# The low part of a conv weight moved from GpSimd to VectorE, and six loads moved behind the next raw weights, in a hybrid attention, Fourier and conv block

## The chip, the core and the metric

The kernel runs on one core of a Trainium2 chip. The core has five engines with instruction queues of their own, which meet only through semaphores: TensorE (PE: matrix products, with a second row PEld for loading the stationary operand), VectorE (DVE), ScalarE (ACT), GpSimd (POOL) and SyncE (SP), from whose queue nearly all DMA transfers are issued. The time is that of one execution on the device, in microseconds (us); lower is better.

## The reference

One layer over 1024 latent tokens and 256 context tokens of width 1024, all in float32, cut to what matters here:

```python
h  = rms_norm(x, g_pre) * (1 + scale) + shift          # latent
hc = rms_norm(ctx, g_pre) * (1 + scale_c) + shift_c     # context
q, k, v, g_a, u_f, g_f, c_a, c_b, g_c, s_a, s_f, s_c = split(h @ w_in)
kc, vc = split((hc @ w_in)[:, 512:1536])
y_a = (neighbourhood_attention(q, k, v, kc, vc, rpb) * silu(g_a)) @ p_attn
y_f = ((real(fft2(u_f)) @ w_four) * silu(g_f)) @ p_four
y_c = (conv_module(c_a, c_b, ...) * silu(g_c)) @ p_conv    # c_a * sigmoid(c_b), depthwise conv of 31 taps, ...
merged = sigmoid(s_a) * y_a + sigmoid(s_f) * y_f + sigmoid(s_c) * y_c
out = x + gate * rms_norm(merged @ w_out, g_post)
```

## The kernel before

Every product is made of three: an operand is split into a high part (rounded, made by ACT as a cast) and a low part (source less high part, a subtraction on POOL or DVE), and `mm3` (L140 to L143) adds high x high (L141), then the two mixed products (L142, L143), in PSUM. `split` (L93) issues one cast and one subtraction. The low part goes to the engine that is named, and to POOL where none is.

**Weights** pass through a queue `wq`. `wreq` and `wcol` enter a weight with the number of pieces `parts` that it is split in and, as `lo`, the engines that make the low parts. `emit_raw` (L108) loads the raw weight into a ring of two buffers (`raw`), `emit_split` writes `whi` and `wlo`, rings of two as well. So a raw load waits until both parts of the weight two places ahead have been made, and the high part of a weight waits until PE has finished the weight two places ahead.

**The stage of the first change** ("border", some 67 to 224 us). PE's order is written out by hand; a scheduler that lists instructions by priority orders ACT, DVE, POOL and SP. PE makes the two Fourier maps (`i_uf`), the second channel tile of the map `c_b` (`i_cb1`, the weight that is changed; its raw buffer is `raw2`, its parts `whi2` and `wlo2`), then the values (`v00`, ...), context keys (`k0`, ...) and the Fourier transform. Into the products of the conv map PE mixes eight pairs of transposes of the context (`tp`, L704); ACT turns each into `h` (L706) and a high part `ch`, POOL makes the low part `cl`. `h` and the transposes have rings of two. Meanwhile DVE runs the depthwise conv: chains of multiply-adds ("taps", L485) with two accumulators, `cacc` (even taps) and `cb_` (odd taps), each 128x512 or 513, joined in L500 to L504. In `fold` (L734, L735) DVE makes `e32` and `o32` from a Fourier map `ut`; ACT and POOL split them (`eh`, `el`, `oh`, `ol`). The weights `wf`, `bc` and `bs` are split by ACT and POOL too (`l_wf`, `l_bc`, `l_bs`). PE multiplies them into four small products, whose low part `wcl` DVE makes; the products take turns in two PSUM buffers, so the third waits for the first `wcl`.

**The stage of the second change** (pairs of gate tiles, about 510 to 745 us). All engines run in the order of the code. Twelve pairs of weight tiles are multiplied with seven products each instead of eight: `step(n, what)` makes the products `p1` to `p7` of pair `n` and the sums `g2`, `g3`, `g4`, `g7`, from which gates are made. `prep_a` to `prep_d` and `wsum` make the stationary operands from the raw weights (`c<-raw` and `w<-raw` in the profile); `raws(n)` loads the two raw tiles of pair `n`, into the same ring of two. `emit_th` writes the tanh of a gate into a ring of two (`th`, L1323) and stores it to DRAM (`thd`, L1324). Pairs 5 to 7 instead multiply their gate into the merge rows `mg[0, 1, 4..7]` (L1340) and store them to `fcd` (L1341). These rows are loaded from `fcd` beforehand: the six loads that are moved, 512 KB each. Up to then the `mg` buffers hold sums of the normalised input (`h_sums`, `h_last`), which are no longer needed at either place.

After the pairs, the branch outputs are projected, merged (`mg`), multiplied with `w_out` and normalised.

Of the kernel before, what the change touches and what calls it, by code (L numbers as in the profile page):

```python
# [19 lines left out]
P = 128  # L20
# [3 lines left out]
KT = D // P  # L24
# [11 lines left out]
Q0, K0, V0, GA0, UF0, GF0, CA0, CB0, GC0, SA0, SF0, SC0 = (  # L36
    0, 512, 1024, 1536, 2048, 2304, 2560, 2816, 3072, 3328, 4352, 5376,
)
# [14 lines left out]
def block_kernel(ctx: ExitStack, tc: tile.TileContext, x, ctxt, wmodp, wgate,  # L53
                 rows2, cols, w_in, rpbp, w_four, w_pw, pst, w_out, masks, bdc, bds, dcos, dsin, out):
    nc = tc.nc
    pe, act, dve, pool, sp = nc.tensor, nc.scalar, nc.vector, nc.gpsimd, nc.sync
# [12 lines left out]
    fcd = dpool.tile([8, P, T], F32, name="fcd")  # L69
# [30 lines left out]
    def wreq(ap, k, n, parts=1, lo=None):  # L100
        wq.append([ap, k, n, None, None, None, parts, lo])
        return len(wq) - 1

    def emit_raw(i):
        while state["raw"] <= min(i, len(wq) - 1):
            e = wq[state["raw"]]
            t = wp.tile([P, e[1], e[2]], F32, tag="raw", bufs=2, name=f"raw{state['raw']}")
            sp.dma_start(t, e[0])  # L108
            e[3] = t
            state["raw"] += 1  # L110
# [26 lines left out]
    def wcol(c0, parts=1):  # L137
        return wreq(w_in[:, c0:c0 + P].rearrange("(k p) c -> p k c", p=P), KT, P, parts)
# [30 lines left out]
    i_s = [[0, 0, 0] for _ in range(8)]  # L169
    i_v, i_kc, i_dft = [[0, 0], [0, 0]], [0] * 4, [[0, 0], [0, 0]]  # L170
    i_uf = [wcol(UF0 + c * P, 4) for c in range(2)]
    i_cb1 = wcol(CB0 + P)
    border = "v00 k0 v01 k1 v10 k2 v11 k3 d0 s0 d1 d2 s1 d3".split()
    for what in border:
        n = int(what[1])
# [1022 lines left out]
    mg = [mgt[d // 4][:, d % 4] for d in range(8)]  # L1198
# [85 lines left out]
    def prep_b(n, which=(0, 1)):  # L1284
        if (n, "c1") not in ops:
            ops[n, "c1"] = [slot(12 + i, f"c1{n}").rearrange("p (k c) -> p k c", k=8) for i in range(2)]
        for i in which:
            put(n, f"s{i + 1}", ops[n, i], ops[n, "c1"], i)
# [13 lines left out]
    def raws(n):  # L1302
        emit_raw(pairs[n - 1][2][1] + 2)
# [135 lines left out]
    def go(n, *what):  # L1439
        for w in what:  # L1440
            step(n, w)
# [40 lines left out]
    go(0, "g7")  # L1482
    h_split(4, 2, 3)
    go(1, "g7")
    for r in (6, 7, 4, 5, 0, 1):
        sp.dma_start(mg[r], fcd[r])
    go(2, "p6", "g2")
    wsum(2, 2)
    wsum(2, 3)
# [12 lines left out]
    prep_d(3)  # L1502
    prep_b(3)
    raws(4)
    go(2, "p3")
    go(3, "p1")
    go(2, "g3")
# [384 lines left out]
```

## Time and profile before

| | us |
|---|---|
| median of 3 runs (930.76 to 933.38) | 930.91 |
| the profiled execution | 931.39 |
| its span, first to last instruction | 929.5 |
| PE busy / DVE busy / ACT busy / POOL busy | 889.4 / 708.3 / 417.3 / 289.4 |
| mean granted TensorE clock | 0.986 of full speed |

How to read the rows. A row of the timeline has start (us from the span's start), duration, engine, line, operation, out<-in by the program's names, shape, count; in brackets the idle time of the engine ahead of it and what released it. Durations of instructions of one engine overlap a little, so that the distance of starts tells the pace. A DVE or POOL instruction's duration holds the time for which it waits after its start. A row of the windows has the stretch and its length, then for PE, PEld, DVE, ACT and POOL busy us and number of instructions, then granted clock, share of the DMA engines in use, GB/s. A row of the waits reads: engine, output and line that waited, releaser; us in total, times, longest.

### The profile page before, as it was taken

Reading aid. Unit: us, or ns where it says so; the run is one execution under the profiler, and the core shown is the slowest. Engines: PE = TensorE matmul, PEld = TensorE weight load, DVE = VectorE, ACT = ScalarE, POOL = GpSimd, SP = SyncE. Lnnn points to the kernel's source line nnn. Section 1 sums busy time; section 2 is a strip of 40 time slices with the busy share of each in tenths; the row PEclk is TensorE's granted clock in tenths of the full one; section 3 lists DMA queues with packets and bytes.
Section 4 is the critical chain, followed back from the end, with each engine's and each line's share of the span. In section 5 each row is a group of like instructions: output and inputs, shape, how many; then the busy total and the mean of one; then the engine's idle time right before and its main releaser. Section 6 shows DMA issues by size and latency. Waiting matters only on the chain. (4 is left out here: it accounts for less than half of the span.)

```text
span 929.5 us, 13195 instructions
## 1 busy us (share of the span) xinstructions
PE 889.4 (96%) x4652; PEld 746.5 (80%) x4652; DVE 708.3 (76%) x1213; ACT 417.3 (45%) x836; POOL 289.4 (31%) x272
## 2 busy tenths in 40 slices
PE   5999999999899999999999999999999999998997
PEld 4677899988678988888888887888888888776685
DVE  5659479582668999999968785667766679998885
ACT  5542523233357676777652544433343530315442
POOL 3026822263234344444521000002300037670232
PEclk9999899999899999999999999999999999999999
DMA  9711133345424554545422238334321798853234
GB/s 367 290 41 68 46 103 126 124 130 180 124 85 141 143 152 127 160 124 143 130 80 91 69 99 281 118 101 125 103 68 46 257 347 311 310 187 104 99 106 136
DMA packets 114163, 135.86 MB, mean 146 GB/s; under 512 B 5681, under 2 KB 83761, under 8 KB 114097
## 3 DMA queue, kind: packets, MB, share of 16 engines
q1 hardware_dynamic: 113952, 134.43, 44.3%
q0 software_dynamic: 144, 0.59, 0.3%
q8 instruction: 37, 0.61, 0.3%
q14 instruction: 30, 0.24, 0.1%
HBM read 102.03 MB, written 29.36 MB: 141 GB/s over the span
## 5 line engine op out<-in xcount | busy, mean ns | idle before, releaser
L141 PE MATMUL ps<-hh,whi 128*128 128x512 f32 x304 | 128.2, 422 | 0.9 <-DVE qd L866 0.9
L93 POOL TENSOR_TENSOR wlo<-raw,whi 128x512 fp32r<-128x512 f32 (+2 forms) x53 | 89.3, 1701 | 117.6 <-ACT whi L93 105.5
L143 PE MATMUL ps<-hh,wlo 128*128 128x512 f32 x304 | 121.0, 398 | 4.7 <-POOL wlo L93 4.7
L142 PE MATMUL ps<-hl,whi 128*128 128x512 f32 x304 | 120.6, 397 | 0.0
L1657 POOL TENSOR_TENSOR mg<-mg,th 128x512 f32<-128x512 f32 x28 | 47.6, 1701 | 99.4 <-DVE th L1654 98.0
L93 ACT CAST whi<-raw 128x512 fp32r<-128x512 f32 (+2 forms) x65 | 43.7, 704 | 74.1 <-PE ps L142 29.7
L143 PEld LDWEIGHTS ps<-hh,wlo 128*128 128x128 f32 x304 | 58.3, 192 | 18.4 <-POOL wlo L93 5.6
L1340 POOL TENSOR_TENSOR mg<-mg,th 128x512 f32<-128x512 f32 x12 | 17.7, 1473 | 167.7 <-DVE th L1339 167.7
L93 DVE TENSOR_TENSOR c<-w,c 128x512 fp32r<-128x512 f32 x64 | 45.9, 756 | 30.4 <-ACT c L93 30.4
L141 PEld LDWEIGHTS ps<-hh,whi 128*128 128x128 f32 x304 | 58.4, 192 | 11.1 <-PE ps L143 1.3
L142 PEld LDWEIGHTS ps<-hl,whi 128*128 128x128 f32 x304 | 58.6, 193 | 9.9 <-issue 0.5
L1028 POOL TENSOR_TENSOR bias<-mk,braw 128x288 f32<-128x288 bf16 (+1 forms) x64 | 54.1, 847 | 38.8 <-DVE mn L1060 37.6
L1093 ACT CAST pt<-tp 96x384 fp32r<-96x384 f32 (+1 forms) x96 | 46.1, 514 | 43.0 <-PE tp L1086 42.1
L1099 DVE TENSOR_TENSOR pt<-tp,pt 96x384 fp32r<-96x384 f32 (+1 forms) x96 | 54.4, 593 | 2.9 <-ACT pt L1093 1.5
L1060 DVE CUSTOM_DVE_ANT_0 pr<-scb,bias 128x544 f32<-128x544 f32 (+1 forms) x64 | 49.4, 772 | 8.4 <-PE scb L1053 7.7
L1067 ACT ACTIVATE pr<-pr,mn 128x544 f32<-128x544 f32 (+1 forms) x64 | 50.8, 794 | 3.7 <-DVE mn L1060 3.6
L143 PE MATMUL ps<-gh,wlo 128*128 128x512 f32 x128 | 50.0, 390 | 0.7 <-DVE wlo L93 0.7
L141 PE MATMUL ps<-gh,whi 128*128 128x512 f32 x128 | 50.3, 393 | 0.0
L142 PE MATMUL ps<-gl,whi 128*128 128x512 f32 x128 | 49.9, 390 | 0.2 <-DVE gl L93 0.2
L1086 PE MATMUL tp<-ident,pr 128*128 128x128 f32 (+1 forms) x320 | 45.8, 274 | 1.4 <-DVE rc L1073 1.0
L93 ACT CAST c<-w 128x512 fp32r<-128x512 f32 x64 | 37.0, 619 | 22.6 <-DVE w L1281 22.3
L1074 DVE TENSOR_SCALAR pr<-pr,rc 128x544 f32<-128x544 f32 (+1 forms) x64 | 41.7, 651 | 2.3
(496 smaller groups left out, 2562.1 us busy)
## 6 DMA issues: line engine op xcount, KB each, us to landing
raw<-in_w_in_dram SPq DMA_DIRECT2D x51, 512.0 KB
wt<-in_wmodp_dram SPq DMA_DIRECT2D x16, 512.0 KB
thd<-th SPq DMA_DIRECT2D x32, 256.0 KB
th<-thd SPq DMA_DIRECT2D x32, 256.0 KB
braw<-in_rpbp_dram SPq DMA_DIRECT2D x32, 192.0 KB
vt<-vd SPq DMA_DIRECT2D x48, 128.0 KB
vd<-vs SPq DMA_DIRECT2D x20, 256.0 KB
vt<-vd SPq DMA_DIRECT2D x48, 96.0 KB
```

The costliest lines, as they stand in the source:

```text
L93: return act.copy(hi, src), (lo_eng or pool).tensor_tensor(out=lo, in0=src, in1=f32(hi), op=ALU.subtract)
L141: pe.matmul(ps, wh, mh, start=start, stop=False, **kw)
L142: pe.matmul(ps, wh, ml, start=False, stop=False, **kw)
L143: pe.matmul(ps, wl, mh, start=False, stop=stop, **kw)
L1028: pool.tensor_tensor(out=dst, in0=mk[:, a * 3 + MJ[j], 0:n].rearrange("p (r w) -> p r w", w=W), in1=raws[h_, min(j, 1)][:, :, 0:W], op=ALU ...
L1060: dve.tensor_tensor_reduce(out=pr, in0=sc, in1=biases[h_][:, FULL[h_](n)], scale=1.0, scalar=BIG, op0=ALU.add, op1=ALU.min, accum_out=mn)
L1067: act.activation(pr, pr, AF.Exp, scale=-1.0, bias=mn, accum_out=sums)
L1074: dve.tensor_scalar(out=pr, in0=pr, scalar1=rc, scalar2=None, op0=ALU.mult)
L1086: pe.transpose(tp[0:(kw if b < 3 else P), b], src, ident)
L1093: act.copy(pt[0:q, b0:b1, 0], tp[0:q, b0:b1])
L1099: dve.tensor_tensor(out=pt[0:q, b0:b1, 1], in0=tp[0:q, b0:b1], in1=f32(pt[0:q, b0:b1, 0]), op=ALU.subtract)
L1657: eng.tensor_tensor(out=mg[d][:, s], in0=mg[d][:, s], in1=t, op=ALU.add)
```

## The change

The low part of the weight `i_cb1` is made by DVE, and both parts in four pieces of 128x256 instead of one of 128x1024. The six loads of merge rows stand behind `raws(4)`.

```diff
     i_uf = [wcol(UF0 + c * P, 4) for c in range(2)]
-    i_cb1 = wcol(CB0 + P)
+    i_cb1 = wreq(w_in[:, CB0 + P:CB0 + 2 * P].rearrange("(k p) c -> p k c", p=P), KT, P, 4, [dve])
...
     go(0, "g7")
     h_split(4, 2, 3)
     go(1, "g7")
-    for r in (6, 7, 4, 5, 0, 1):
-        sp.dma_start(mg[r], fcd[r])
     go(2, "p6", "g2")
     wsum(2, 2)
     wsum(2, 3)
     go(2, "p5")
     prep_c(2)
     go(0, "p4")
     prep_d(2)
     raws(3)
     go(0, "g4")
     go(1, "p4", "g4")
     go(2, "p7")
     prep_a(3)
     go(2, "p4", "g7", "g4")
     for i in range(4):
         wsum(3, i)
     prep_d(3)
     prep_b(3)
     raws(4)
+    for r in (6, 7, 4, 5, 0, 1):
+        sp.dma_start(mg[r], fcd[r])
     go(2, "p3")
```

What the scheduler makes of the first edit on DVE, in the border stage. Before, the two accumulators alternate for a long stretch (twenty rows ahead of these are alike), then come the folds and the second piece of the value weight (`wlo3`):

```order
L485 SCALAR_TENSOR_TENSOR cacc0_696<-u0_694,colt_70,cacc0_696 128x513
L485 SCALAR_TENSOR_TENSOR cb__710<-u0_694,colt_70,cb__710 128x512
L734 TENSOR_TENSOR e32_1064<-ut0_756 128x511
L735 TENSOR_TENSOR o32_1065<-ut0_756 128x511
L93 TENSOR_TENSOR wlo3_971<-raw3_878,whi3_970 128x512
L500 SCALAR_TENSOR_TENSOR cacc0_696<-cacc0_696,colt_70,cb__710 128x512
```

Now five even taps in a row come ahead of the first piece `wlo2`; a tap follows each piece, and the odd taps that are left stand in a row of seven behind the folds (shown from the last piece on):

```order
L485 SCALAR_TENSOR_TENSOR cacc0_696<-u0_694,colt_70,cacc0_696 128x513 x5
L93 TENSOR_TENSOR wlo2_875<-raw2_808,whi2_874 128x256
...
L485 SCALAR_TENSOR_TENSOR cacc0_696<-u0_694,colt_70,cacc0_696 128x513
L485 SCALAR_TENSOR_TENSOR cb__710<-u0_694,colt_70,cb__710 128x512
L734 TENSOR_TENSOR e32_1070<-ut0_756 128x511
L735 TENSOR_TENSOR o32_1071<-ut0_756 128x511
L485 SCALAR_TENSOR_TENSOR cb__710<-u0_694,colt_70,cb__710 128x512 x7
L93 TENSOR_TENSOR wlo3_977<-raw3_884,whi3_976 128x512
```

The number of taps is the same, but seven of them now depend each on the one directly ahead. PE's order is unchanged, POOL only loses the one subtraction, ACT's one cast becomes four with a copy of a Fourier map after the first.

On SP, in the stage of pairs, before (`raw37` and `raw38` are the weights of pair 3, `raw39` and `raw40` those of pair 4):

```order
L1324 DMA thd_59<-th_6166 128x512
L1486 DMA mg1_5659<-fcd_58 128x1024 x4
L1486 DMA mg0_5658<-fcd_58 128x1024 x2
L1324 DMA thd_59<-th_6190 128x512
L108 DMA raw37_6234<-in_w_in_dram 128x8x128
L108 DMA raw38_6236<-in_w_in_dram 128x8x128
L1324 DMA thd_59<-th_6239 128x512
```

and now:

```order
L108 DMA raw37_6234<-in_w_in_dram 128x8x128
L108 DMA raw38_6236<-in_w_in_dram 128x8x128
L1324 DMA thd_59<-th_6239 128x512
L1324 DMA thd_59<-th_6256 128x512
L1324 DMA thd_59<-th_6293 128x512
L1324 DMA thd_59<-th_6297 128x512
L108 DMA raw39_6317<-in_w_in_dram 128x8x128
L108 DMA raw40_6319<-in_w_in_dram 128x8x128
L1504 DMA mg1_5665<-fcd_58 128x1024 x4
L1504 DMA mg0_5664<-fcd_58 128x1024 x2
L1324 DMA thd_59<-th_6355 128x512
L1324 DMA thd_59<-th_6378 128x512
```

Both pairs of raw weights and five tanh stores now go ahead of the six loads; the two tanh stores of the last rows now stand behind them.

## The prediction

> **What bounds the kernel now.** The page comes first: its table of busy time says which engine's time is the kernel's time.
>
> ```profile
> PE 889.4 (96%) x4652; PEld 746.5 (80%) x4652; DVE 708.3 (76%) x1213; ACT 417.3 (45%) x836; POOL 289.4 (31%) x272
> ```
>
> TensorE (PE) is busy for 889 of 929.5 us, so only what makes it wait, or run slowly, can be won. The waits of PE, longest first, are the second view (us in total, times, longest). Two rows touch the change, and a third stands close behind it.
>
> ```profile
> PE ps L143 <- POOL wlo L93: 4.7, 2, 3.8
> PE x L141 <- ACT c L93: 2.9, 2, 1.7
> ...
> PE ps L141 <- DVE wcl L93: 1.0, 1, 1.0
> ```
>
> The third view, the timeline, gives the places. First the wait on `wlo`, on PE:
>
> ```profile
> 88.36 0.38 PE L704 MATMUL tp<-ident,x 128*128 128x128 f32 x2
> 89.99 0.38 PE L704 MATMUL tp<-ident,x 128*128 128x128 f32 x2
> 90.45 0.40 PE L142 MATMUL ps<-hl,whi 128*128 128x512 f32 x1
> 94.68 0.79 PE L143 MATMUL ps<-hh,wlo 128*128 128x512 f32 x1 [3.84 <-POOL wlo L93]
> 100.82 0.40 PE L143 MATMUL ps<-hh,wlo 128*128 128x512 f32 x1
> ```
>
> One round (a pair of context transposes and six products) takes 89.99 - 88.36 = 1.63 us, and a product 0.23. The product at 94.68 was due at 90.68: 4.0 us lost. From 94.68 to 100.82 lie exactly two rounds, 3.26 us of work, and they took 6.14. The windows view gives the reason: the granted clock (the number before the last two) is half there.
>
> ```profile
> 94.68:100.82 6.14, 6.14 (x17) 4.76 (x17) 2.30 (x3) 4.68 (x10) 5.53 (x8) 0.50 0.35 96
> 571.00:575.40 4.40, 4.31 (x11) 3.17 (x12) 4.19 (x7) 2.75 (x6) 0.00 (x0) 0.61 0.46 171
> ```
>
> So the wait cost 4.0 + 2.88 = 6.9 us. Why `wlo` came late stands in the rows of POOL, DVE and ACT.
>
> ```profile
> 79.49 15.13 POOL L93 TENSOR_TENSOR wlo<-raw,whi 128x1024 fp32r<-128x1024 f32 x1 [3.47 <-ACT whi L93]
> 130.25 2.41 POOL L93 TENSOR_TENSOR wlo<-raw,whi 128x1024 fp32r<-128x1024 f32 x1 [2.29 <-ACT whi L93]
> 94.71 1.41 POOL L93 TENSOR_TENSOR cl<-h,ch 128x256 fp32r<-128x256 f32 x2
> 109.15 1.30 POOL L93 TENSOR_TENSOR ol<-o,oh 128x512 fp32r<-128x512 f32 x1
> ...
> 77.88 0.75 DVE L485 SCALAR_TENSOR_TENSOR cacc<-u,colt,cacc 128x513 f32<-128x513 f32 x1
> 91.74 0.69 DVE L735 TENSOR_TENSOR o<-ut 128x511 f32<-128x511 f32 x1
> 98.48 0.71 DVE L93 TENSOR_TENSOR wlo<-raw,whi 128x512 fp32r<-128x512 f32 x1 [6.05 <-ACT whi L93]
> 121.96 0.42 DVE L93 TENSOR_TENSOR wcl<-ps,wch 128x256 fp32r<-128x256 f32 x1
> ...
> 78.36 1.05 ACT L93 CAST whi<-raw 128x1024 fp32r<-128x1024 f32 x1 [3.47 <-issue]
> 95.47 0.56 ACT L706 ACTIVATE h<-tp,mods 128x256 f32<-128x256 f32 x1 [7.29 <-POOL cl L93]
> ```
>
> The same subtraction that takes 2.41 us elsewhere took 15.13 here. It ended 2.2 us after DVE's unbroken row of convolution taps ended (91.74 + 0.69 = 92.43): POOL stood still while DVE ran taps end to start. Where the taps depend on each other the two take turns:
>
> ```profile
> 194.59 1.74 POOL L93 TENSOR_TENSOR wlo<-raw,whi 128x512 fp32r<-128x512 f32 x1
> 195.22 1.66 DVE L485 SCALAR_TENSOR_TENSOR cacc<-u,wsum,cacc 128x512 f32<-128x512 f32 x1
> 156.78 6.28 DVE L485 SCALAR_TENSOR_TENSOR cacc<-u,colt,cacc 128x513 f32<-128x513 f32 x8
> ```
>
> A turn of both takes 1.7 us, of which POOL's 128x512 is 1.25 (1.30 less the overlap with the next) and DVE's tap 0.47. Alone, dependent taps come every 6.28 / 8 = 0.79. The Trainium skill (SBUF — State Buffer, Who interferes with whom) calls this an exclusive lock between GpSimd and VectorE instructions with two SBUF inputs, in which the loser blocks; it speaks against the change, since work moved from one of these engines to the other stays behind the same lock. The trace agrees, in the 15.13 us above.
>
> The second place is PE at 569, where pair 3 of the gate tiles begins:
>
> ```profile
> 569.01 0.39 PE L143 MATMUL z<-hh,c 128*128 128x512 f32 x1
> 571.09 0.50 PE L141 MATMUL x<-hh,c 128*128 128x512 f32 x1 [1.70 <-ACT c L93]
> 575.56 0.39 PE L143 MATMUL x<-hh,c 128*128 128x512 f32 x1
> ...
> 539.73 1.14 ACT L93 CAST c<-raw 128x512 fp32r<-128x512 f32 x2 [0.38 <-DMA raw<-in_w_in_dram]
> 568.70 0.63 ACT L1323 ACTIVATE th<-u 128x512 f32<-128x512 f32 x1 [6.88 <-DMA thd<-th]
> 570.42 1.14 ACT L93 CAST c<-raw 128x512 fp32r<-128x512 f32 x2 [1.09 <-DMA raw<-in_w_in_dram]
> ...
> 535.57 0.99 SPq L108 DMA_DIRECT2D raw<-in_w_in_dram  x2
> 556.84 2.84 SPq L1486 DMA_DIRECT2D mg<-fcd  x6
> 560.38 4.40 SPq L108 DMA_DIRECT2D raw<-in_w_in_dram  x2
> ...
> 560.00:570.00 10.00, 9.40 (x42) 7.46 (x40) 2.52 (x4) 1.26 (x2) 0.00 (x0) 1.00 1.04 358
> ```
>
> The product due at 569.24 began at 571.09 (1.85 lost); eleven products to 575.56 took 4.47 us instead of 11 x 0.23 = 2.5 (1.97 lost, at the clock of 0.61 above). The raw weights it waits for were issued at 560.38 behind the six `mg` loads, with the DMA engines full (share 1.04, the last but one number), and landed 10 us later; without `mg` ahead, those issued at 535.57 were there at 539.7, in 4.1 us. Together 3.8 us.
>
> **Part 1: the weight's low part on DVE.** POOL loses one 128x1024 subtraction, 2.2 us behind the lock. ACT makes the high part in four casts of at most 0.56 (`h` above has 128x256 too), up to 1.2 us more than the one of 1.05, on an engine that waits at this place anyway. The pieces stand behind five chained taps, which from 77.88 at 0.79 each end at 81.8. Instructions that don't depend on the one ahead follow each other at 0.66 (21 from 77.88 to 91.74), a piece of 128x256 at half of that: the four pieces with three taps between them end at 85.1, or, each at its full 0.42 and 0.79, at 85.9. PE needs them from 90.68 on. The wait of 4.0 and its half clock go: 6.9 us. SP gains: its next raw load waited for this subtraction to free its buffer, and comes 9 us earlier; nobody waited for it.
>
> What is late next? Eight more instructions follow on DVE that don't depend on the one ahead (taps and the first fold), at 0.66, to 90.2, and POOL's first `cl` (ready at 86.6) must wait for it. ACT's `h` of round k waits for `cl` of round k-2, as 95.47 shows, and the transpose of round k for `h` of round k-2. With a `cl` of 0.62 and a tap of 0.47 per turn, `cl` 0 to 3 end at 90.8, 91.9, 93.0, 96.4 (a piece of the value weight lies between the last two), and transposes 5 and 7 wait 0.3 and 0.4 us. PE stays 6.9 - 0.7 = 6.2 us ahead, say 6.0 with the semaphores.
>
> But the lock's row decides what follows. From 90.2 until `ol` is done (109.15 + 1.24 = 110.4 before) it must hold, in turns: 13 DVE instructions (six taps, the value weight's piece, one tap, L500, L504, L502, L490, L466) at 0.47 = 6.1, and on POOL eight `cl` at 0.62 (5.0), one value piece (1.25), `l_wf` (1.25), `l_bc` and `l_bs` (0.8), `el` and `ol` (2.5), a short copy (0.1): 10.9. The end is 107.2, only 3.2 earlier. Everything up to `wcl` follows in the old distance: the second fold, its splits, the tanh for the second half of the conv map, the taps. `wcl` then ends at 122.4 - 3.2 = 119.2, and PE is at this product 6.0 earlier:
>
> ```profile
> 121.15 0.28 PE L143 MATMUL ps<-whi,hl 128*128 128x256 f32 x1
> 122.44 0.38 PE L141 MATMUL ps<-h_wf,h_bs 128*128 128x256 f32 x1 [1.01 <-DVE wcl L93]
> ```
>
> It would be due at 121.27 - 6.0 = 115.3 and waits until 119.25: 4.0 us, as long as the wait removed. A wait of that length cost 2.9 us of half clock, which I take again. Part 1: -3.2 + 2.9 = -0.3 us.
> The unknown is the tap's share of a turn. At 0.47 the chain ends 3.2 earlier; at the 0.79 of lone taps the 13 instructions take 10.3 and it ends 1.0 later. The place is like 195.22, so I take 0.47 and keep both: part 1 from -3.2 + 2.9 to +1.0 + 2.9.
>
> **Part 2: the six `mg` loads.** On SP they move behind one tanh store, the raws of pair 3, four tanh stores and the raws of pair 4. They wait for nothing at either place. The raws of pair 3 can then go when their buffers are free: after `w` (558.1) and after `c` (560.5), both on DVE.
>
> ```profile
> 557.43 0.69 DVE L1281 TENSOR_TENSOR w<-raw,w 128x512 f32<-128x512 f32 x1
> 559.86 0.69 DVE L93 TENSOR_TENSOR c<-raw,c 128x512 fp32r<-128x512 f32 x1
> ...
> L1340 POOL TENSOR_TENSOR mg<-mg,th x12: 1289/1414/1681, 619.8 to 675.0; 128x512 f32<-128x512 f32 x12
> ```
>
> In 4.1 us they land at 562.2 and 564.6; ACT's cast (0.6) and DVE's subtraction (0.7) are done by 564, 5 us before PE needs them at 569.24. ACT's wait of 6.88 for a tanh buffer goes too, as that store is no longer behind `mg`. So -3.8 us. What is moved back: the raws of pair 4 go at about 570.5, `mg` from 571.5 on (2.84 to issue, some 9 us to land by the 10 above, so until 584), and two tanh stores behind them land at about 584. ACT takes the first of those buffers again after pair 3's seventh product, at 586: 2 us to spare, and a late tanh there holds up nothing on PE for another 5. `mg` itself is first read at 619.8, 35 us later. Cost nothing.
>
> **Sum.** -0.3 - 3.8 = -4.1 us against the profiled execution (931.39 us, span 929.5, 1.9 around it), that is 927.3. It lies 0.5 over the median of 930.91, to which the same difference gives 926.8.
>
> **Rivals.** (a) PE does not wait for `wcl`: the chain keeps up with PE, part 1 is -6 and the total -10: 921. Against it: 17 us of work behind one lock. (b) It waits as computed, but the clock stays: -3.2 - 3.8 = -7: 924. The wait at 571 pulled the clock down after only 1.7 us, one of 1.0 at 122.44 did not, so this needs a `wcl` wait near 1 us or luck. The Trainium skill (TensorE: Matmul & The Clock Gate, What's actually happening) puts the drop at an idle window of about 3.4 us; by that, a wait shortened to 2 or 3 us would already bring this case. (c) Turns go badly: POOL is held off as at 79.49, the chain is up to 1.0 later, half clock on top: +3.9 - 3.8, about 931, no change. (d) Slower: the half clock after `wcl` outlasts the 6.1 us seen. Each us of it costs 0.47 (2.88 / 6.14); with gains of 7.0 it decides from 15 us on, and at 22 us gives 934. DVE is at its busiest there, which feeds short waits on PE; but the low stretches shown above ended after 6.1 and 4.4 us. (e) The `mg` loads were not what held the raws: part 2 gives nothing, total -0.3: 930.6; against it stand 10 us against 4.1.
>
> **How the numbers follow.** A measurement here can tell about 0.3% (2.8 us) from no change, so faster means under 928.1. The forecast, within 925 to 928.5: 0.47. (a) 0.11; (b) 0.19; (c) 0.14; (d) 0.03; (e) 0.06. Faster: (a), (b) and nine tenths of the forecast, 0.73; slower (d), 0.03; the same 0.24. The range leaves out (d), (e), half of (a) and a third of (c), 0.19 in all: 921.5 to 930.3.
>
> **What would show it.** In the profile after: no PE wait on `wlo` near 91, and four DVE rows `wlo` 128x256 by 86; short PE waits on `h` at the transposes; PE's wait on `wcl` of about 4 us near 119 with a granted clock of 0.5 behind it; `ol` ended near 107. At 569 (less what part 1 moved) no wait and full clock, ACT's `c` waiting for no DMA, the `mg` loads in SP's rows behind the second pair of raws. The prediction is wrong if PE waits for `cl` for more than 2 us, if the `wcl` wait stays at 1 us, or if a tanh buffer stops PE after 580.

## The result, and the profile after

The changed kernel took 926.01 us (median of 14 runs, 924.53 to 930.23), the kernel before 931.36 (14 runs on the same chip, 929.62 to 933.95). The ratio is 0.9948, 95% interval 0.9938 to 0.9958: 0.5% faster, against a forecast of 926.8. The profiled execution took 925.71 us (span 924.0), 5.7 less than the one of before.

From the list of PE's waits after: the wait of 3.8 on the conv weight's `wlo` is gone (the 0.9 left is a later weight's, and stood beside it before), that on `x<-c` of 1.7 too, and the wait on `wcl` has grown from 1.0.

```profile
PE ps L141 <- DVE wcl L93: 5.4, 1, 5.4
...
PE ps L143 <- POOL wlo L93: 0.9, 1, 0.9
```

The timeline after at the first place, by engine (PE, DVE, POOL, ACT). This execution runs 0.64 us later than the one of before up to here (first context transpose at 85.79, before at 85.15), 0.5 of it from a longer first wait of PE.

```profile
85.79 0.38 PE L704 MATMUL tp<-ident,x 128*128 128x128 f32 x2
97.09 0.38 PE L704 MATMUL tp<-ident,x 128*128 128x128 f32 x2
120.52 0.58 PE L141 MATMUL ps<-h_wf,h_bs 128*128 128x256 f32 x1 [5.37 <-DVE wcl L93]
...
85.65 0.42 DVE L93 TENSOR_TENSOR wlo<-raw,whi 128x256 fp32r<-128x256 f32 x1
89.24 1.23 DVE L485 SCALAR_TENSOR_TENSOR cb__710<-u,colt,cb__710 128x512 f32<-128x512 f32 x1
105.43 1.78 DVE L502 SCALAR_TENSOR_TENSOR cacc<-cacc,colt,cb__710 128x512 f32<-128x512 f32 x1
108.40 0.68 DVE L734 TENSOR_TENSOR e<-ut 128x511 f32<-128x511 f32 x1
120.05 0.42 DVE L93 TENSOR_TENSOR wcl<-ps,wch 128x256 fp32r<-128x256 f32 x1
...
87.30 3.77 POOL L93 TENSOR_TENSOR cl<-h,ch 128x256 fp32r<-128x256 f32 x2 [6.89 <-ACT ch L93]
89.88 2.33 POOL L93 TENSOR_TENSOR cl<-h,ch 128x256 fp32r<-128x256 f32 x2
104.90 1.76 POOL L93 TENSOR_TENSOR ol<-o,oh 128x512 fp32r<-128x512 f32 x1
...
109.17 0.62 ACT L93 CAST eh<-e 128x512 fp32r<-128x512 f32 x1 [8.41 <-DVE e L734]
```

The last of the four pieces is done at 86.07. The eight pairs of transposes, 85.79 to 97.09, follow at an even 1.61 us: no wait on `h` at all. The third small product then stands for 5.37 us until `wcl`, which ends at 120.47. The windows view tells what follows: half clock for some five us, and, at the second place, full clock.

```profile
120.50:126.50 6.00, 5.98 (x30) 5.98 (x31) 2.61 (x5) 0.52 (x2) 0.00 (x0) 0.56 0.01 3
569.00:577.00 8.00, 8.00 (x37) 6.60 (x37) 5.50 (x9) 4.03 (x8) 0.00 (x0) 1.00 0.82 257
```

At that second place the timeline shows the raw weights of pair 3 issued when their buffers come free, the `mg` loads behind the raws of pair 4, and ACT's casts (`c<-raw`) with no wait for a DMA:

```profile
558.41 0.38 SPq L108 DMA_DIRECT2D raw<-in_w_in_dram  x1
560.84 0.38 SPq L108 DMA_DIRECT2D raw<-in_w_in_dram  x1
570.23 1.01 SPq L108 DMA_DIRECT2D raw<-in_w_in_dram  x2
571.29 3.68 SPq L1504 DMA_DIRECT2D mg<-fcd  x6
...
562.31 0.63 ACT L1323 ACTIVATE th<-u 128x512 f32<-128x512 f32 x1 [0.23 <-DVE u L1344]
562.85 1.12 ACT L93 CAST c<-raw 128x512 fp32r<-128x512 f32 x2
...
L1340 POOL TENSOR_TENSOR mg<-mg,th x12: 1289/1414/1678, 615.7 to 670.8; 128x512 f32<-128x512 f32 x12
```

The first use of `mg` moved from 619.8 to 615.7, with PE. Where the 5.5 us of span went: at 188 us PE stands 0.4 behind the trace of before (that is 0.26 ahead, less the late start); from there to 615.7 it gains 4.5; the last 1.4 come at 844, where the same wait of 1.6 on `c` was followed by half clock in the one trace and not in the other (last section), so they are not the change's.

For the first place the best yardstick is a length that a late start doesn't touch: from the first context transpose to the first product of the Fourier stage (`eo`), the same work in all kernels.

```profile
187.94 0.28 PE L141 MATMUL eo<-whi,ah 128*128 128x256 f32 x1
```
```profile
188.32 0.28 PE L141 MATMUL eo<-whi,ah 128*128 128x256 f32 x1
```

Before (first row) it is 187.94 - 85.15 = 102.8, after (second row) 188.32 - 85.79 = 102.5. This length is called the stage below.

### The profile page after: what moved, and what is told of

It is laid out like the page before. It is cut to its first block, busy times and chain, and to the rows that moved or that the text cites. A ratio compares the mean times of both kernels' runs of the same rounds, so it can differ in the third digit from the quotient of the medians.

```text
span 924.0 us, 13202 instructions
## 1 busy us (share of the span) xinstructions
PE 885.0 (96%) x4652; PEld 744.9 (81%) x4652; DVE 716.0 (77%) x1217; ACT 417.6 (45%) x839; POOL 281.0 (30%) x271
## 5 line engine op out<-in xcount | busy, mean ns | idle before, releaser
L93 POOL TENSOR_TENSOR wlo<-raw,whi 128x512 fp32r<-128x512 f32 (+2 forms) x52 | 74.4, 1449 | 116.8 <-ACT whi L93 116.7
```

Of the source, the lines that this page charges most:

```text
L93: return act.copy(hi, src), (lo_eng or pool).tensor_tensor(out=lo, in0=src, in1=f32(hi), op=ALU.subtract)
```

## The experiments

Where a run was timed, its ratio is to the kernel before, run beside it on the same chip (931.37 for the first four, 932.51 for the next three); of the other four (e8 to e11) there is one time and a trace, with the kernel before at 928.0 beside the last three.

**One edit alone.** `e1_weight_only` has the first edit, `e2_loads_only` the second.

```diff
 # e1: the kernel before with
-    i_cb1 = wcol(CB0 + P)
+    i_cb1 = wreq(..., KT, P, 4, [dve])
```

> The kernel before with only the first edit: the low part of the conv weight in four pieces on VectorE; the mg loads stay. Theory (the wait on wlo became one on wcl): the wait of 4.0 us at 90.7 and its half clock (2.9) go, the wait of about 5.4 on wcl at 115 and half clock behind it (about 2.6) come, so 0 to -1 us, 930.4 to 931.4; PE waits at 569 as before. Rival (this edit carries the gain): about 927.

Measured: 931.17 us, ratio 0.9995 (0.998 to 1.0011); stage 101.9; the wait on `wcl` 5.33, and 1.9 us lost to half clock behind it. As the theory had it.

```diff
 # e2: the kernel before with
     go(1, "g7")
-    for r in (6, 7, 4, 5, 0, 1):
-        sp.dma_start(mg[r], fcd[r])
...
     raws(4)
+    for r in (6, 7, 4, 5, 0, 1):
+        sp.dma_start(mg[r], fcd[r])
```

> The kernel before with only the second edit: the six mg loads behind raws(4); the weight's low part stays on GpSimd in one piece. Theory (the loads' bytes held up the raw weights of pair 3): the wait at 569 and its half clock go, -3.8 to -4.4 us, 927.0 to 927.6; the wait on wlo at 90.7 stays. Rival (this edit gives nothing, the first gives all): 931.

Measured: 927.23 us, ratio 0.9948 (0.993 to 0.9966), so -4.8 us, with -3.2 and -6.5 as the ends; no wait at 569. The second edit makes the whole difference. But one sentence of the expectation failed: the wait on `wlo` did not stay. From the timeline (POOL, DVE, PE):

```profile
80.21 2.39 POOL L93 TENSOR_TENSOR wlo<-raw,whi 128x1024 fp32r<-128x1024 f32 x1 [3.13 <-ACT whi L93]
...
80.28 2.88 DVE L485 SCALAR_TENSOR_TENSOR cacc<-u,colt,cacc 128x513 f32<-128x513 f32 x1
...
120.81 0.58 PE L141 MATMUL ps<-h_wf,h_bs 128*128 128x256 f32 x1 [5.54 <-DVE wcl L93]
```

Up to 500 us this is the kernel before, instruction for instruction. Yet here POOL had the lock at once, the subtraction took 2.39 instead of 15.13, DVE's tap waited for it (2.88 instead of 0.75), and PE waited 5.54 for `wcl`, as after the change. So the kernel before was run again for a second trace of its own.

> The kernel before once more, for its trace. Theory (whether GpSimd is held off by the taps is decided anew in each execution, and wcl decides the time either way): either wlo takes about 15 us, PE waits 4 us for it and about 1 for wcl, or wlo takes 2.4 us and PE waits about 5.4 us for wcl; the third small product starts at 121 to 123 us in both. Rival (the lock goes the same way each time): wlo takes about 15 us again.

Measured: 930.45 us; the stage is 102.5. From its timeline (POOL, PE):

```profile
80.67 15.16 POOL L93 TENSOR_TENSOR wlo<-raw,whi 128x1024 fp32r<-128x1024 f32 x1 [3.45 <-ACT whi L93]
...
95.89 0.80 PE L143 MATMUL ps<-hh,wlo 128*128 128x512 f32 x1 [3.87 <-POOL wlo L93]
123.31 0.39 PE L141 MATMUL ps<-h_wf,h_bs 128*128 128x256 f32 x1 [1.98 <-DVE wcl L93]
```

POOL was held off again. The same instructions, then, either take 15 us or 2.4, and the stage is as long either way: 102.8 and 102.5 held off (the two traces of the kernel before), 102.5 not (e2), and 101.9 to 102.5 with the first edit (after, e1, e7). That is why the first edit is worth nothing: `wcl` comes at 120.5 to 123 whoever waits first, and PE's wait is only taken at another place.

**What holds `wcl`?** DVE is the one late. (POOL has a part in that: after the change, a tap ahead of `wcl`, at 112.90, took 2.88 instead of 0.75 beside a weight's subtraction that POOL had begun at 112.38. No run moved that subtraction.) Two kernels attack the wait from both sides: one gives PE other work ahead of it, one takes taps out of DVE's queue.

```diff
 # e3: the changed kernel, in the loop over the small products
             wch[si][k] = (hi, lo)
-            adv(2)
+            adv(6 if (si, k) == (0, 1) else 2)
```

> The changed kernel with six steps of value and context-key products instead of two on PE between the second and the third small product of the DFT weights (54 products of 0.12 us each more, 6.5 us). Theory (the wait on wcl took back the first edit's gain): PE reaches the third product at about 121.5, behind wcl at 120.1, so the wait of 5.4 and the half clock of 2.6 go: -8 us, about 918. Rival (VectorE is the bound of the whole stage, and the next product that needs it waits instead): 926.

Measured: 924.12 us, ratio 0.9922 (0.9903 to 0.9942); stage 101.8, 0.7 shorter than after the change. The gain of 8 did not come. PE, ACT and DVE in its timeline:

```profile
121.92 0.39 PE L141 MATMUL ps<-h_wf,h_bs 128*128 128x256 f32 x1 [1.02 <-DVE wcl L93]
127.72 0.58 PE L142 MATMUL ps<-wlo,hh 128*128 128x256 f32 x1 [4.35 <-DVE wlo L93]
...
118.05 1.14 ACT L93 CAST whi<-raw 128x512 fp32r<-128x512 f32 x2 [5.21 <-PE ps L143]
...
122.44 2.85 DVE L485 SCALAR_TENSOR_TENSOR cb__710<-u,colt,cb__710 128x512 f32<-128x512 f32 x1
126.99 0.68 DVE L93 TENSOR_TENSOR wlo<-raw,whi 128x512 fp32r<-128x512 f32 x1
```

The rival held: the wait moved to the next thing that DVE owes PE, the second piece of the next value weight. Its high part was ready at 119.2; its low part stood until 126.99 behind taps, one of which was itself held off by POOL (2.85).

```diff
 # e4: the changed kernel, ahead of the context rounds
-    tap["rate"] = 1.0
+    tap["rate"] = 0.0
```

> The changed kernel with no convolution taps asked for during the eight context rounds (rate 0.0 instead of 1.0); they come later, none is left out. DVE's order then has the second fold and the tanh product ahead of the last taps of the first channel, and wcl eight instructions behind it. Theory (DVE's queue ahead of wcl is what PE waits for): wcl ends at 112 to 115, before PE needs it, -8 us, about 918. Rival (the taps put off, some 11 us of DVE, come back between 130 and 160 us, where DVE is 90% busy): PE waits there instead, 924 to 928.

Measured: 925.47 us, ratio 0.9936 (0.9915 to 0.9958); stage 104.7. `wcl` did come earlier, and the wait on the value weight took its place again, behind the taps that were put off:

```profile
116.63 0.39 PE L141 MATMUL ps<-h_wf,h_bs 128*128 128x256 f32 x1 [1.26 <-DVE wcl L93]
130.60 0.58 PE L142 MATMUL ps<-wlo,hh 128*128 128x256 f32 x1 [4.53 <-DVE wlo L93]
...
125.18 4.43 DVE L485 SCALAR_TENSOR_TENSOR cacc<-u,colt,cacc 128x513 f32<-128x513 f32 x3
129.86 0.68 DVE L93 TENSOR_TENSOR wlo<-raw,whi 128x512 fp32r<-128x512 f32 x1
```

So neither is enough alone. The next kernel does both, and puts most taps off until 128 us.

```diff
 # e5: the changed kernel, ahead of the context rounds
-    tap["rate"] = 1.0
+    tap["rate"] = 0.5
 # ahead of the folds
-    tap["rate"] = 0.5
+    tap["rate"] = 0.0
 # in the loop over the small products
-            adv(2)
+            adv(6 if (si, k) == (0, 1) else 2)
```

> The changed kernel with the six steps between the second and the third small product (as in the run with more work ahead of wcl) and fewer taps asked for: rate 0.5 instead of 1.0 with the context rounds, 0.0 instead of 0.5 around the folds and the small products; none is left out, they run after 130 us. DVE then makes the first wcl behind two taps of the second channel instead of six, and the second piece of the next value weight directly behind the second wcl. Theory (what PE waits for between 115 and 130 us is DVE's queue of taps, held up further by the shared lock, first ahead of wcl, then ahead of wlo): neither wait is left, the 5.4 us and the half clock of 2.6 us go, -8 us against 926.0: 918, within 1.5. Rival (the stage is short of DVE time as a whole, so that the waits only move behind 130 us): 923 to 926.

Measured: 920.62 us, ratio 0.9884 (0.986 to 0.9909), the fastest of all kernels here. In its profiled execution (917.34 us) PE's timeline has no wait between 85 and 179 us, and DVE does what PE needs early:

```profile
112.64 0.75 DVE L93 TENSOR_TENSOR wcl<-ps,wch 128x256 fp32r<-128x256 f32 x2
118.65 1.37 DVE L93 TENSOR_TENSOR wlo<-raw,whi 128x512 fp32r<-128x512 f32 x1 [5.26 <-ACT whi L93]
...
85.19 0.38 PE L704 MATMUL tp<-ident,x 128*128 128x128 f32 x2
179.81 0.28 PE L141 MATMUL eo<-whi,ah 128*128 128x256 f32 x1
```

The stage is 94.6, 7.9 us shorter than after the change: the 8 us that the theory gave. It holds 46 taps instead of 57, so the others come behind it. The median is 2.6 over the forecast of 918 and outside its 1.5, so part of the gain is given back later in some executions. A second trace was taken for that.

> The kernel with fewer taps and more work once more, for its trace: its six times lie in two groups, three at 917.3 to 919.2 and three at 922.0 to 924.0. Theory (granted clock): an execution at 922 to 924 differs in half clocks behind waits of 1.5 us and more (each some 1.7 to 3.4 us), at 233 or 831 us. Rival (something moves in the order of waits near 115 to 130): a wait of 3 us and more there. If it falls in the fast group it tells nothing of this.

Measured: 920.24 us, between the groups; stage 94.7, no wait in it. It lost 1.71 at a wait on `kst`, whose low part DVE makes and which the profiled execution at 917.34 hardly waits for (0.2), and, at 832, half clock behind the wait of 1.54 on `c` that the other trace has at full clock. From its timeline, and from its windows from that product on:

```profile
228.32 0.47 PE L141 MATMUL ps<-hh,whi 128*128 128x512 f32 x1 [1.71 <-DVE kst L557]
```
```profile
832.38:836.00 3.62, 3.62 (x11) 2.63 (x12) 3.62 (x6) 2.47 (x3) 0.00 (x0) 0.74 0.08 14
```

These two, 1.5 and 1.7 us, account for the 2.9 us between the two executions; what those at 922 to 924 have on top was not seen. A wait on `kst` stands only in the four traces with taps put off in this way (e5, e6, e9, e10: 0.2 to 5.6), so it is likely the price of putting them off.

**What is the first edit worth where `wcl` no longer decides?** The same kernel with the old weight.

```diff
 # e6: e5 with
-    i_cb1 = wreq(..., KT, P, 4, [dve])
+    i_cb1 = wcol(CB0 + P)
```

> The kernel of the run with fewer taps and more work, but with the conv weight as before: low part by GpSimd in one piece. Theory (GpSimd is starved only in some executions; one profile of the old weight had it, another not): the median lies 0 to 3 us above that of the run with fewer taps, its runs spread more widely, since the wait on wlo and its half clock, 6.9 us, now come through in the executions that have it. Rival (the wait on wlo comes in every execution, and the trace without it was an accident): about 6.9 us above, 925. Second rival (it hardly ever comes): the same time.

Measured: 921.83 us, ratio 0.9904 (0.9873 to 0.9935), six runs of 918.6 to 927.16 against e5's 917.34 to 924.03. The intervals overlap: the difference of 1.2 is not resolved. In the profiled execution `wlo` took 2.72 and the stage 94.6. A second trace:

> The kernel with fewer taps, more work and the old weight once more, for its trace. Theory (GpSimd is held off by the taps in some executions only; two of four traces of the old weight so far): if wlo takes about 15 us again, PE waits some 4 us at 91, and with no wait on wcl behind it that stays, 924 to 927; if it takes 2.4 to 2.7, 918 to 922. Rival (held off or not, the time is the same): 919 to 922 with a wlo of 15 us.

Measured: 927.61 us, though `wlo` took only 2.61. This time POOL lost the lock one instruction later, at the first `cl`. POOL and PE:

```profile
79.84 2.61 POOL L93 TENSOR_TENSOR wlo<-raw,whi 128x1024 fp32r<-128x1024 f32 x1 [2.91 <-ACT whi L93]
87.00 6.47 POOL L93 TENSOR_TENSOR cl<-h,ch 128x256 fp32r<-128x256 f32 x1 [3.96 <-ACT ch L93]
...
94.12 0.69 PE L704 MATMUL tp<-ident,x 128*128 128x128 f32 x2 [2.03 <-ACT h L706]
236.10 0.77 PE L141 MATMUL ps<-hh,whi 128*128 128x512 f32 x1 [5.58 <-DVE kst L557]
```

The `cl` took 6.47, PE waited 2.03 for `h` (and 1.7 of half clock), and the stage is 98.4: 3.8 longer, and this time it stays. With the wait on `kst`, 5.58 here, the execution is 7.4 us behind e9. So neither theory had the place right: with a `wlo` of 2.61, 918 to 922 was expected. But where nothing waits for `wcl`, being held off costs stage time: it did so in one of the two traces with the old weight, and in neither of the two with the new one (e5, e9). How often it comes, so few traces can't tell.

**The engine or the pieces?** e11 is the changed kernel with the four pieces on POOL.

```diff
-    i_cb1 = wreq(..., KT, P, 4, [dve])
+    i_cb1 = wreq(..., KT, P, 4, [pool])
```

> The changed kernel with the four pieces made by GpSimd instead of VectorE; the taps stand again in their long row with alternating accumulators. Theory (the engine matters, not the pieces): the first piece is held off for the rest of DVE's row of taps in some executions, until about 93, then PE waits some 4 us at 91; in others each piece takes 0.6 to 0.7 and PE waits 5.4 for wcl; the time is 925 to 927 either way. Rival (short pieces slip in between taps): never held off; PE waits for wcl alone.

Measured: 925.02 us; stage 103.0. The first piece alone was held off for the rest of the row, as POOL's timeline shows:

```profile
78.69 14.15 POOL L93 TENSOR_TENSOR wlo<-raw,whi 128x256 fp32r<-128x256 f32 x1 [2.84 <-ACT whi L93]
```

Short pieces did not slip in. PE waited 2.21 for `wlo`, 2.04 for `h` at 96.37 and 1.23 for `wcl`, with 6.83 us at half clock from 93.73 on. So pieces on POOL can be held off as one long subtraction was; that the engine settles it rests on this one execution and the seven in which DVE made them.

**The loads: bytes or queue?** With the first edit in, the six loads at their old place, from POOL's queue.

```diff
-        sp.dma_start(mg[r], fcd[r])
+        pool.dma_start(mg[r], fcd[r])
```

> The kernel before with the first edit, and the six mg loads at their old place in the program, but issued from GpSimd's queue instead of SyncE's; GpSimd does nothing else there. Theory (the 3 MB of the loads fill the DMA engines while the raw weights of pair 3 are due): the raws are issued a little earlier but still land late, PE waits at 569 as before: 930 to 931. Rival (it is the place in SyncE's queue that held the raws up): no wait at 569, 926.5 to 927.5.

Measured: 927.63 us, ratio 0.996 (0.9946 to 0.9973). The time is the rival's but for 0.1 us, the reason is neither's. From POOL, SP, ACT and PE in the timeline:

```profile
549.62 2.72 POOL L1486 DMA_DIRECT2D mg<-fcd  x5 [59.42 <-DVE t L93]
...
561.11 0.53 SPq L108 DMA_DIRECT2D raw<-in_w_in_dram  x1
563.62 0.38 SPq L108 DMA_DIRECT2D raw<-in_w_in_dram  x1
...
560.04 0.63 ACT L1323 ACTIVATE th<-s 128x512 f32<-128x512 f32 x1 [4.70 <-DMA thd<-th]
...
561.72 0.50 PE L141 MATMUL x<-t,c 128*128 128x512 f32 x1 [1.53 <-ACT c L93]
```

With nothing ahead of them in that queue, the loads went 7 us earlier than before (556.84), and five of the six had landed when the first raw was issued. The raws were not issued earlier than before (560.38), and yet came in time. Now the one who is late is a tanh store, for whose buffer ACT waits 4.70 and PE, behind ACT, 1.53; the DMA engines' share was 1.00 from 555 to 561. The loads are no longer ahead of that store in its queue, and it is late all the same: the 3 MB in the DMA engines are enough to hold up whoever has a transfer due just then. Whether the place in SyncE's queue adds anything beyond setting the time, no run shows.

## Why the prediction was right, step by step

**Right in sum and, in the main, in mechanism.** Forecast -4.1; measured -5.4 by the medians, of which the first edit alone gave -0.2 (forecast -0.3) and the second alone -4.1 (forecast -3.8); by the ratios -4.8, of which -0.5 and -4.8. Within the intervals the two simply add. The wait at 91 came back at `wcl` with its half clock, as the sum had it. That the parts agree to within half a microsecond is luck in part: terms were off and cancelled, and both parts hold a half clock that other executions have shorter or not at all.

**Part 1, where the sizes were off and cancelled.** Times of after, as far as `ol`, are given here less the late start of 0.64. The pieces ended at 85.4, as forecast (85.1 to 85.9). POOL's first `cl` was held off, but to 88.6 and not to 90.2: the first tap that POOL slowed is the one at 89.24 in the rows above (1.23). So the first `cl` ended 1.5 us sooner than forecast, the transposes never waited (forecast 0.7), and PE was 6.9 ahead instead of 6.0. POOL was through with `ol` at 106.0, 4.4 earlier than before and not 3.2 (forecast 107.2). The step that failed is the next: "Everything up to `wcl` follows in the old distance". Before, DVE had nothing left but the second fold, which waited for `el` and ran beside `ol`:

```profile
109.22 1.76 DVE L734 TENSOR_TENSOR e<-ut 128x511 f32<-128x511 f32 x1 [4.10 <-POOL el L93]
```

It was done 0.5 after `ol`. Now DVE was itself still at the end of its list (in the rows of after, L502 at 105.43, then L490 and L466), came to the fold at 108.40 and was done with it 2.4 after `ol`. That took back 1.9 of the 4.4: in distance from the first transpose, `wcl` let PE go on 2.6 us earlier (34.73 against 37.29), not 3.2. PE's wait was therefore 5.37 instead of 4.0, and the half clock behind it 2.6 instead of 2.9: -2.6 + 2.6 = 0.

**A premise that the prediction took from one trace.** "POOL stood still while DVE ran taps end to start" was read as what the row of taps does. It is what it does in some executions (before, e8, e11), not in others (e2, e6), where the two take turns beside the same alternating taps. The sum survived because the wait on `wcl` fills in whatever the wait on `wlo` leaves.

**Part 2.** The raws, the casts and the tanh stores went as worked out; no PE wait between 540 and 600, and no tanh buffer late after 580. Measured by place (188 to 616 us), 4.5 us against 3.8: beside the 1.85 and 1.97 summed there, a wait of 0.25 on `u` at 587 is gone as well, which with its restart cost 0.5. But the 1.97 of half clock is not a fixed price. With the loads at the old place, e1 and e8 waited only 1.26 and 1.44 on `c`, had no half clock behind it, and waited 1.80 on `u` at 586 instead (e8 with half clock behind that). From the product at 555.64 to the one at 598.08 (times of before), PE took 42.4 us before, 43.8 in e8 and 42.0 in e1, but 38.1 after and in e2: the second edit is worth 3.9 to 5.7 there, whichever way the loss is taken.

**The rivals.** (a) and (b) are out: PE waited, at a clock of 0.56. (c) is out: POOL was held off for 1.9 us, within the forecast. (d) is out: the low clock ended 5.3 us after PE went on. (e) is out by e2.

## What to carry to other kernels

Before a wait is taken away, look for the next one behind it: here POOL's `wlo` stood in front of `wcl`, and `wcl` in front of the next `wlo`, and only with DVE's taps out of the way of both (e5) did PE keep the 8 us. A long wait in one trace may be a throw of the dice: a second trace of the same program can tell whether it is a cost or an accident. And a load that isn't needed for 35 us belongs where nothing else is due, which a full DMA share beside a waiting engine shows at a glance.

## What the runs showed of the hardware

**Who gets the shared lock is decided anew in each execution.** With GpSimd's subtractions beside the alternating taps, one of them took 15.13, 15.16 and 14.15 us (before, e8, e11) or 6.47 (e10's `cl`), and the first took 2.39 and 2.72 in two other executions, e2 and e6. In the first three, POOL stayed off until DVE came to the end of its unbroken row; in e10 it came in behind the fold at 92.21. Where DVE made the pieces, in seven traces, the longest delay was that of the first `cl` after, some 1.9 us. What tips it was not found: POOL's start stood 0.28 us behind the start of a tap in the trace of before, which lost, and in e6, which won.

**Half clock behind short waits depends on where they fall.** Over the 13 traces, by the mean clock of the 8 us behind a PE wait that has no longer one within 5 us: after waits of 0.9 to 1.3 us the clock never fell (30 of 30); after 1.4, at one place near the start (18 to 20 us), it fell in 10 of 13; after 1.4 to 2.1 elsewhere in 6 of 23; after 2.2 to 2.9 in 13 of 13, 12 of them at one place in the layer norm, where PE has little to do; after 3.8 to 5.8 in 9 of 9. Only behind the first wait of the program (8.4 to 9.7 us) the profile shows full clock in all 13. The loss was 1.4 to 3.4 us and did not grow with the wait: 1.4 after 5.76, 1.7 after 1.58. The wait of 1.58 and 1.59 on `c` near the end, before and after the change, from the first product behind it:

```profile
843.68:847.50 3.82, 3.82 (x10) 2.77 (x11) 3.82 (x6) 2.46 (x3) 0.00 (x0) 0.66 0.27 30
```
```profile
839.60:844.00 4.40, 4.38 (x18) 3.33 (x19) 4.40 (x6) 3.54 (x5) 0.00 (x0) 1.00 0.19 59
```

0.66 against 1.00: this alone is 1.7 us between two executions that differ in nothing there. The granted clock itself shows why the loss does not grow with the wait. But for the one at the end of the program, every low stretch lasted 3.41 us or twice that, and within one execution all of them begin on one grid of 3.41 us: in the trace of before at 18.89, 93.98, 240.75, 571.85 and 844.91, which lie 22, 65, 162 and 242 steps behind the first. The stretch at 844.91:

```profile
844.91:848.32 3.41, 3.41 (x9) 2.66 (x9) 3.41 (x5) 1.56 (x2) 0.00 (x0) 0.50 0.36 49
```

Where PE stood idle for less than 1.2 us in one step of this grid, none of 2505 steps at full clock was followed by a low one; with 1.2 to 2.0 us, 15 of 36 were; with more, 26 of 26 (from 10 us on, 13 traces). So a wait is at risk once 1.2 us of it lie within one step, and the same wait in another execution, which meets the grid elsewhere, may be spared; what decides between 1.2 and 2.0 stays open. The Trainium skill (TensorE: Matmul & The Clock Gate, What's actually happening) puts the drop at an idle window of about 3.4 us. The traces agree for waits above that, but for the first of the program, and differ below: a wait of 1.54 was enough once, one of 1.98 was not.
